# Down projection of a two-layer decoder: ten steps of the second block product moved ahead of the first's last step, other memory for the last sums, final norm of four tiles in halves

## The chip, the cores and the metric

The kernel runs on one core of one Trainium2 chip. The metric is the device time of one execution in microseconds; of several runs the median is taken. The engines are named as in the profile: PE (TensorE matmul), PEld (its weight loads), DVE (VectorE), ACT (ScalarE), POOL (GpSimd) and SP (SyncE, which here only issues DMAs; SPq in the profile's rows).

## The reference

Two decoder layers on a sequence of 1024 rows of width 1024 in float32, each ending in a gated feed-forward block, and a final norm. The attention parts, which the change does not touch, are left out here:

```python
def conv_ffn(h, w_up, conv_w, conv_b, w_down):
    u = h @ w_up                                   # 1024 x 5632
    u = causal_depthwise_conv3(u, conv_w) + conv_b
    a, b = u[..., :D_FF], u[..., D_FF:]            # D_FF = 2816
    return (jax.nn.silu(a) * b) @ w_down           # the down projection
...
for l in range(2):
    ...
    x = x + concat(o_mix, o_mem) @ w_o[l]
    x = x + conv_ffn(rms_norm(x, ffn_norm[l]), w_up[l], conv_w[l], conv_b[l], w_down[l])
return rms_norm(x, final_norm)
```

`rms_norm(x, g)` is x / sqrt(mean(x²) + 1e-6) · g over the 1024 columns of a row.

## The kernel before

**Precision.** A float32 matmul is done as three matmuls on a split of each operand into a high and a low part (`mm3`, lines 157 to 159). The split itself is one ACT instruction (high part, line 81) and one DVE subtraction (low part, line 82). Both operands of the subtraction lie in SBUF.

**The block products.** The down projection is a matrix product in 2x2 blocks done with seven block products instead of eight (the Winograd variant of Strassen's scheme). Class `Down` holds it. Its hidden dimension (2 x 11 tiles of 128) is cut in halves, so each block product has NK = 11 accumulation steps; a step (i, j) is 4 row tiles x 3 matmuls of 128x128x512, 12 matmuls in all. `PRODUCTS` names, for each of the seven products i, the index of its left operand among seven stored factors, its right operand (a tile of `w_down` or a sum of such tiles), whether it adds on into the four running PSUM banks ("chain") or has banks of its own, and which blocks of the output it goes to. Product 0 uses factor 0 and the weights b11; product 1 uses factor 1 and b21. `steps` is the order of all 77 steps: all of product 0, then all of product 1, and so on.

**The left operands.** The gated hidden tiles come out of class `Up` two at a time. `gate` (line 1351, DVE) forms g; `left(k)` (lines 1359 to 1362, POOL) makes for pair k four sums and differences of halves, s1, s2, g12 and s4, into three small tiles (tag `gs`, three buffers) and g itself; `store(k)` (line 1368) writes the seven factors to DRAM with seven DMAs in the order g, h, s2, g12, h12, s1, s4. Factors 0 and 1 are halves of g and h and need no sum. The last pair is k = 10, which step (i, 10) of every product reads.

**Fetch and split.** `fetch` (line 1456) reads the left operands back from DRAM in pairs of steps into a rotating raw buffer (`wr`, three buffers), and stops at a pair whose factors are not stored yet. `prep` splits the operands of a step into four rotating buffers (`wh`, `wl`), three steps ahead of the matmuls. The DMAs of `store`, of `fetch`, of the weights (`claim`, line 1445) and of the rows x (line 1122) are all issued by SP, which works off its queue in order.

**Weight sums.** `sums` makes the sums of weight tiles that later products need, one DVE instruction for each step of products 1 to 4 (lines 1477, 1479, 1481 and the next): `t3 = b22 - b12` belongs to product 1, `b11 = t3 + b11` to product 2, `b12 = b22 - b11` to product 3. Both inputs lie in SBUF.

**The order of instructions.** Inside `Up.run` the order on DVE and ACT is written out by slots; the first seven down steps (slots 160 to 166) and `store(10)` (slot 166) fall in it. Around and after it, a list scheduler fixes each engine's order when the kernel is compiled: it takes the first instruction in program order that its own time model holds to be ready. So a weight sum that is ready can be put in much earlier than the step that it belongs to. On the chip each engine works in that fixed order.

**The end.** `add` (line 1509, DVE) adds the PSUM banks of a finished product to x. Product 6, the last, goes to the left 512 columns of row tiles 4 to 7. `final(t)` is the last norm of row tile t: ACT squares 1024 columns with their sum (line 118), DVE scales the sum (line 119), POOL takes the power -0.5 (line 121), DVE multiplies (line 1094), SP stores 512 KB (line 1095). Its result tile `xn` has three buffers. Tiles 0 to 2 are done during product 5, tiles 3 to 7 after the last step in program order.

Of the kernel before, what the change touches and what calls it, by code (L numbers as in the profile page):

```python
# [8 lines left out]
F32 = mybir.dt.float32  # L9
F32R = mybir.dt.float32r  # L10
BF16 = mybir.dt.bfloat16
AF = mybir.ActivationFunctionType
ALU = mybir.AluOpType
# [4 lines left out]
P = 128  # L18
D = 1024
S = 1024  # L20
NT = S // P
KT = D // P
CH = 512
# [6 lines left out]
NF = DFF // P  # L30
QSC = HD ** -0.5
EPS = 1e-6
# [10 lines left out]
class Trunk:  # L43
    def __init__(self, ctx, tc, a, out):
        self.tc, self.nc, self.a, self.out = tc, tc.nc, a, out
        e = ctx.enter_context
        self.cp = e(tc.tile_pool(name="cp", bufs=1))
        self.wp = e(tc.tile_pool(name="wp", bufs=1))
        self.hp = e(tc.tile_pool(name="hp", bufs=1))
        self.pp = e(tc.tile_pool(name="pp", bufs=1, space=PSUM))  # L50
        self.dp = e(tc.tile_pool(name="dp", bufs=1, space=DRAM))
        self.uid = 0
# [152 lines left out]
    def load_block(self, w, cols, gcol=None, step=2, pool=None):  # L205
        tiles = [self.load_rows(w, k0, min(step, KT - k0), cols, gcol, pool) for k0 in range(0, KT, step)]

        def at(kt, c0, n):
            hi, lo = tiles[kt // step]
            return hi[:, kt % step, c0:c0 + n], lo[:, kt % step, c0:c0 + n]  # L210
        return at
# [230 lines left out]
    def attention(self, ap, l, od, units, work, spare, lead=4, lag=2, lead_work=2):  # L442
# [79 lines left out]
        for k in range(first, len(steps) + lag + 4):  # L522
            st = steps[k] if 0 <= k < len(steps) else None
            run(k, "max")
            if st:
                self.turn_p(ap, st)
            run(k, "exp")
            if st:
                self.lower_p(st)
            run(k, "norm")  # L530
            while items and items[0]["at"] <= k:
                begin(k, items.pop(0))
            if k < 0 and lead_work and items:
                for _ in range(lead_work):
                    if work:
                        advance()
            if st and k < n_fill:
                owed += max(total, 0) / (n_fill - k)
                while owed >= 1 and work:
                    owed -= 1  # L540
                    advance()
            if 0 <= k - lag < len(steps):
                self.value(steps[k - lag])
                if steps[k - lag]["end"]:
                    finish(k, steps[k - lag]["u"])
            if not work and whole and k % 4 == 0:
                operand()
            if k == units[-1]["start"]:
                w_o = self.load_block(self.a["w_o"][l], [(0, CH)])
# [539 lines left out]

    def final(self, pool, gb, t):  # L1090
        nc = self.nc
        xn = self.sb(pool, [P, D], F32, "xn", 3)
        r = self.rstd(pool, self.x[:, t, :], xn)
        nc.vector.scalar_tensor_tensor(xn, self.x[:, t, :], r, gb, ALU.mult, ALU.mult)
        nc.sync.dma_start(self.out[0, t * P:(t + 1) * P, :], xn)

    def residual(self, pool, src):
        self.x = pool.tile([P, NT, D], F32, name=self.nm("x"))
        for t in range(NT):
            self.nc.sync.dma_start(self.x[:, t, :], src[t * P:(t + 1) * P, :])  # L1100
# [11 lines left out]
                up.run(late, down)  # L1112
        return down

    def down_all(self, l, down, pool, each, last):

        self.x = pool.tile([P, NT, D], F32, name=self.nm("x"))
        for n in range(down.at_step, len(down.steps)):
            i, j = down.step()
            if 11 <= n < 27 and n % 2:  # L1120
                t = n // 2 - 5
                self.nc.sync.dma_start(self.x[:, t, :], self.xm[l][t * P:(t + 1) * P, :])
            if i == 5:
                each(j)
            if n == len(down.steps) - 1:
                last()
            if j == down.NK - 1:
                down.add(i)
# [45 lines left out]
    def run(self):  # L1174
        a, tc = self.a, self.tc
        self.constants()
        self.xd = self.dp.tile([S, D], F32, name="xd")
        self.xm = [self.dp.tile([S, D], F32, name=f"xm{l}") for l in range(2)]
        oT = self.layer1_attn(*self.middle(self.layer0()))
        with tc.tile_pool(name="fx1", bufs=1) as fx:  # L1180
            down = self.gated(1, oT, self.xd, fx)
            with tc.tile_pool(name="y1", bufs=1) as yp:
                gb = []

                def each(j):
                    if j == 0:
                        gb.append(self.gain(yp, a["final_norm"].rearrange("(o n) -> o n", o=1)))
                    if j % 3 == 2:
                        self.final(yp, gb[0], j // 3)
                self.down_all(1, down, yp, each, lambda: None)  # L1190
                for t in range(3, NT):
                    self.final(yp, gb[0], t)


class Up:
# [158 lines left out]
    def left(self, k):  # L1354

        g, h = self.hidden[2 * k:2 * k + 2]
        s1, s2, s4 = (self.k.sb(self.late, [P, CH], F32, "gs", 3) for _ in range(3))
        add = self.k.nc.gpsimd.tensor_tensor
        add(s1, g[:, CH:], h[:, CH:], ALU.add)  # L1359
        add(s2, s1, g[:, :CH], ALU.subtract)  # L1360
        add(g[:, CH:], g[:, :CH], g[:, CH:], ALU.subtract)
        add(s4, h[:, :CH], s2, ALU.subtract)
        self.factors = (g[:, :CH], h[:, :CH], s2, g[:, CH:], h[:, CH:], s1, s4)
# [49 lines left out]
class Down:  # L1413

    NK = NF // 2
# [5 lines left out]
    def __init__(self, k, l, gds, fx):  # L1421
        self.k, self.l, self.gds, self.fx = k, l, gds, fx
        self.w = k.a["w_down"][l]
        NK = self.NK
        self.names = {"x": [("b11", i) for i in range(NK)] + [("t3", i) for i in range(NK)] + [("b22", NK - 1)],
                      "h": [("b21", i) for i in range(NK)] + [(n, i) for i in range(NK) for n in ("b12", "b22")][:-1]}
        self.place = {}
        self.steps = [(i, j) for i in range(7) for j in range(NK)]
        self.pairs = [(i, j, min(2, NK - j)) for i in range(7) for j in range(0, NK, 2)]
        self.ready, self.raws, self.at_step = [], [], 0  # L1430

    def claim_x(self):
# [26 lines left out]
    def prep(self, upto):  # L1459

        k = self.k
        while len(self.ready) < min(upto, len(self.steps)):
            i, j = self.steps[len(self.ready)]
            n = self.PRODUCTS[i][1]
            pair = i * (self.NK + 1) // 2 + j // 2
            self.fetch(pair + 1)
            hi, lo = k.whl([P, 2, CH])
            for x, src in enumerate((self.raws[pair][:, j % 2, :], self.place[n, j])):
                k.split(src, hi[:, x, :], lo[:, x, :])
            self.ready.append((hi, lo))  # L1470
            if j % 2 or j == self.NK - 1:
                self.fetch(pair + 4)
# [9 lines left out]
        elif i == 4:  # L1482
            tt(at["b11", j], at["b21", j], at["b11", j], ALU.subtract)

    def step(self):
        k, n = self.k, self.at_step
        i, j = self.steps[n]
        _, _, run, dst = self.PRODUCTS[i]
        self.prep(n + 1 + self.AHEAD)
        if n == 0:  # L1490
            self.chain = [k.psb() for _ in range(4)]
        if j == 0:
            self.banks = self.chain if run else [t[:, x * CH:(x + 1) * CH] for t in (k.psa(), k.psa()) for x in range(2)]
        hi, lo = self.ready[n]
        first = i == 0 or not run
        for p in range(4):
            ps = slice(p * P, (p + 1) * P)
            k.mm3(self.banks[p], (hi[:, 0, ps], lo[:, 0, ps]), (hi[:, 1, :], lo[:, 1, :]), first and j == 0, j == self.NK - 1, not first)
        self.sums(i, j)
        self.at_step += 1  # L1500
        return i, j

    def add(self, i):

        for banks in ((), (self.banks, self.chain))[i] if i < 2 else (self.banks,):
            for p in range(4):
                for rows, col in self.PRODUCTS[i][3]:
                    xs = self.k.x[:, rows * 4 + p, col * CH:(col + 1) * CH]
                    self.k.nc.vector.tensor_tensor(xs, banks[p], xs, ALU.add)
# [57 lines left out]
```

## Time and profile before

| what | value |
|---|---|
| median of 3 runs | 2588.83 us (2588.57 to 2593.57) |
| the profiled execution | 2594.71 us, of which 2592.9 us lie between its first and its last instruction (the span) |
| PE busy | 2467.9 us, 95% of the span |
| DVE, ACT, POOL busy | 1869.4, 1341.3 and 757.6 us |
| granted TensorE clock, mean | 0.986 |

A row of the timeline reads: start in us, busy time in us, engine, line of the kernel, operation, output tile <- input tiles, shapes, how many instructions are merged, and in square brackets how long the engine had been idle before and what ended that. A row of stretches reads: the stretch, its length, the busy time and count of each engine, the granted clock, the share of the DMA engines' time and the rate.

### The profile page before, as it was taken

How to read it: one execution, taken by the hardware profiler on the slowest of the kernel's cores; microseconds unless marked ns; L12 is line 12 of the kernel's file. 1: busy time of each engine (PE TensorE's matmuls, PEld its weight loads, DVE VectorE, ACT ScalarE, POOL GpSimd, SP SyncE). 2: the span in 40 equal slices, each digit the busy share in tenths (PEclk: the TensorE clock that was granted, in tenths of full speed). 3: DMA queues.
4: the chain of work that ended last, by engine and by line, in shares of the span. 5: the costliest groups of instructions: out<-in, count | busy, mean ns of one | idle time of the engine just before them, and what ended most of it. 6: DMA issues, size and time to landing. Idle time of an engine off the chain costs nothing.

```text
span 2592.9 us, 35691 instructions
## 1 busy us (share of the span) xinstructions
PE 2467.9 (95%) x12306; PEld 2058.8 (79%) x12306; DVE 1869.4 (72%) x3172; ACT 1341.3 (52%) x2553; POOL 757.6 (29%) x616
## 2 busy tenths in 40 slices
PE   7899999988999999998999999999999999998998
PEld 7787877777778888886889888887777888886886
DVE  5758888886477878777765468878376777777765
ACT  4437777885254445443454357767144454453443
POOL 0105445453135455433000000000233445544000
PEclk9999999999999999999999999999999999999999
DMA  8473233345323333366235467666522333337433
GB/s 251 141 210 111 66 98 99 110 123 170 108 74 105 96 108 102 98 222 233 90 125 160 147 181 199 190 180 183 195 90 78 102 102 110 106 98 281 165 98 114
DMA packets 302700, 357.68 MB, mean 138 GB/s; under 512 B 37960, under 2 KB 183224, under 8 KB 302520
## 3 DMA queue, kind: packets, MB, share of 16 engines
q1 hardware_dynamic: 302520, 355.41, 43.4%
q8 instruction: 97, 1.59, 0.3%
q14 instruction: 83, 0.68, 0.1%
HBM read 245.55 MB, written 109.78 MB: 137 GB/s over the span
## 4 chain that ended last, share of the span: by engine, by line
PE 74%; DVE 8%; ACT 6%; DMA 5%; POOL 3%; issue 3%; SPq 0%; POOLq 0%; ACTq 0%; DVEq 0%
PE psa L157 12%; PE psa L158 12%; PE psa L159 12%; PE psb L157 9%; PE psb L159 9%; PE psb L158 9%; PE psb L399 4%; PE psb L422 4%; PE psa L300 4%; DVE pt L409 2%; ACT pt L406 1%; POOL gs L1359 1%; DVE wl L82 1%; DMA hT<-in_w_down_dram 1%; DVE ps L330 1%
## 5 line engine op out<-in xcount | busy, mean ns | idle before, releaser
L81 ACT ACTIVATE wh<-wr 128x512 fp32r<-128x512 f32 (+2 forms) x254 | 192.8, 763 | 358.2 <-PE psb L159 146.3
L82 DVE TENSOR_TENSOR wl<-wr,wh 128x512 fp32r<-128x512 f32 (+2 forms) x254 | 242.5, 959 | 166.2 <-ACT wh L81 165.5
L1344 DVE SCALAR_TENSOR_TENSOR v<-u,cw,v 128x1023 f32<-128x1023 f32 (+1 forms) x176 | 275.4, 1565 | 68.8 <-ACT v L1342 67.2
L409 DVE TENSOR_TENSOR pt<-psb,pt 128x512 fp32r<-128x512 f32 (+2 forms) x380 | 247.1, 660 | 66.7 <-ACT pt L406 63.9
L1342 ACT ACTIVATE v<-u,cw 128x1024 f32<-128x1024 f32 x88 | 109.6, 1245 | 310.2 <-DVE u L1331 283.4
L406 ACT ACTIVATE pt<-psb 128x512 fp32r<-128x512 f32 (+2 forms) x380 | 213.4, 572 | 88.0 <-PE psb L399 82.0
L422 PE MATMUL psb<-pt,vv 128*128 128x512 f32 (+2 forms) x864 | 225.9, 356 | 18.2 <-DVE pt L409 12.2
L157 PE MATMUL psa<-hT,wh 128*128 128x512 f32 x560 | 220.3, 394 | 5.3 <-DVE u L1305 5.3
L159 PE MATMUL psa<-hT,wl 128*128 128x512 f32 x560 | 219.5, 392 | 0.8 <-DVE wl L82 0.8
L158 PE MATMUL psa<-hT,wh 128*128 128x512 f32 x560 | 219.7, 392 | 0.0
L300 PE MATMUL psa<-kk,qq 128*128 128x512 f32 (+4 forms) x792 | 185.1, 348 | 13.3 <-DVE stat L330 7.0
L121 POOL TENSOR_TENSOR rs<-ss,consts 128x1 f32<-128x1 f32 x44 | 25.8, 589 | 514.0 <-DVE ss L119 375.0
L422 PEld LDWEIGHTS psb<-pt,vv 128*128 128x128 f32 x864 | 141.2, 191 | 43.5 <-DVE pt L409 21.0
L343 ACT ACTIVATE ps<-ps,stat 128x128 f32<-128x128 f32 (+1 forms) x192 | 147.8, 771 | 46.5 <-DVE stat L330 46.3
L481 POOL TENSOR_TENSOR wr<-wr 128x512 f32<-128x512 f32 x32 | 41.8, 1309 | 430.5 <-DMA kd<-st 246.2
L1246 POOL TENSOR_TENSOR ws<-wr 128x512 f32<-128x512 f32 x44 | 76.5, 1739 | 296.4 <-DMA wr<-in_w_up_dram 256.6
L157 PE MATMUL psb<-wh 128*128 128x512 f32 x352 | 139.5, 396 | 20.8 <-ACT wh L81 20.7
L157 PE MATMUL psb<-hT,wh 128*128 128x512 f32 x384 | 156.6, 408 | 1.5 <-DVE pt L409 1.4
L399 PE MATMUL psb<-consts,ps 128*128 128x128 f32 x928 | 148.4, 277 | 8.1 <-DVE pt L409 3.4
L159 PE MATMUL psb<-hT,wl 128*128 128x512 f32 x384 | 151.1, 393 | 0.0
L158 PE MATMUL psb<-hT,wh 128*128 128x512 f32 x384 | 150.5, 392 | 0.0
L330 DVE CUSTOM_DVE_ANT_0 ps<-psa,caub 128x128 f32<-128x128 f32 (+1 forms) x192 | 139.0, 751 | 14.9 <-PE psa L300 14.7
(286 smaller groups left out, 6799.7 us busy)
## 6 DMA issues: line engine op xcount, KB each, us to landing
wr<-in_w_up_dram SPq DMA_DIRECT2D x88, 512.0 KB
wr<-gd SPq DMA_DIRECT2D x154, 256.0 KB
gd<-v SPq DMA_DIRECT2D x88, 256.0 KB
gd<-gs SPq DMA_DIRECT2D x66, 256.0 KB
o<-ob SPq DMA_DIRECT2D x128, 128.0 KB
wr<-o SPq DMA_DIRECT2D x32, 512.0 KB
hT<-in_w_down_dram SPq DMA_DIRECT2D x64, 256.0 KB
qd<-st SPq DMA_DIRECT2D x56, 256.0 KB
```

Source lines behind the costliest of these rows:

```text
L81: nc.scalar.activation(hi, src, AF.Copy)
L82: nc.vector.tensor_tensor(lo, src, f32(hi), ALU.subtract)
L157: mm(out, lh, rh, start=first, stop=False, skip_group_check=more)
L158: mm(out, lh, rl, start=False, stop=False, skip_group_check=more)
L159: mm(out, ll, rh, start=False, stop=last, skip_group_check=more)
L300: nc.tensor.matmul(out, w, rhs, start=b not in banks[:i], stop=b not in banks[i + 1:])
L330: self.nc.vector.tensor_tensor_reduce(p, s, br["spans"][ii][2], -1.0, 3e38, ALU.add, ALU.min, br["stat"][:, 0, ii:ii + 1])
L399: nc.tensor.transpose(tp[0:kb, x:x + P], br["pt"][ii][:, o:o + kb], self.ident)
L406: nc.scalar.activation(st["hi"], st["src"], AF.Copy)
L409: self.nc.vector.tensor_tensor(st["lo"], st["src"], f32(st["hi"]), ALU.subtract)
L422: self.nc.tensor.matmul(out, v, t, start=st["begin"] and i == 0, stop=st["end"] and i == len(mms) - 1)
L1344: nc.vector.scalar_tensor_tensor(v[:, d:], u[:, :S - d], cw[:, tap, i:i + 1], v[:, d:], ALU.mult, ALU.add)
```

## The change

There are three parts.

1. In `Down`, the steps of products 0 and 1 get a new order: instead of eleven steps of product 0 and then eleven of product 1, there are ten steps of product 0, ten steps of product 1, then (0, 10) and (1, 10). The pairs that `fetch` reads follow the same order (`pairs`, `pair_of`), and the PSUM banks are kept per product. This holds for both layers.
2. In `Up.left`, the last pair's three sums go to two tiles of the tag `ws` instead of three of the tag `gs`. This holds for both layers too.
3. In the last layer only, steps 9 and 10 of product 6 are merged (`joint`): for each row tile the six matmuls of both steps run together. The final norm of tiles 4 to 7 is split: `final_right` squares the right 512 columns and multiplies them by the gain during product 6, and `final_left` does the left 512 columns after the end, scales the finished right half, and stores two halves. `xn` has two buffers instead of three, `final(3)` stands in product 6, and each of tiles 4 to 7 has a buffer of its own.

```diff
     def final(self, pool, gb, t):
-        xn = self.sb(pool, [P, D], F32, "xn", 3)
+        xn = self.sb(pool, [P, D], F32, "xn", 2)
...
+    def final_right(self, pool, gb, t):
+        nc, x = self.nc, self.x[:, t, CH:]
+        xn = self.sb(pool, [P, D], F32, "xr", 4)
+        ss = self.sb(pool, [P, 3], F32, "sr", 4)
+        nc.scalar.activation(xn[:, CH:], x, AF.Square, accum_out=ss[:, 0:1])
+        nc.vector.tensor_scalar(ss[:, 0:1], ss[:, 0:1], 1.0 / D, EPS, ALU.mult, ALU.add)
+        nc.vector.tensor_tensor(xn[:, CH:], x, gb[:, CH:], ALU.mult)
+        return xn, ss
+
+    def final_left(self, pool, gb, t, xn, ss):
+        nc, x = self.nc, self.x[:, t, :CH]
+        nc.scalar.activation(xn[:, :CH], x, AF.Square, accum_out=ss[:, 1:2])
+        nc.vector.scalar_tensor_tensor(ss[:, 2:3], ss[:, 1:2], 1.0 / D, ss[:, 0:1], ALU.mult, ALU.add)
+        r = self.sb(pool, [P, 1], F32, "rs", 4)
+        nc.gpsimd.tensor_tensor(r, ss[:, 2:3], self.nhalf, ALU.pow)
+        nc.scalar.activation(xn[:, CH:], xn[:, CH:], AF.Copy, scale=r)
+        nc.vector.scalar_tensor_tensor(xn[:, :CH], x, r, gb[:, :CH], ALU.mult, ALU.mult)
+        for n in (1, 0):
+            nc.sync.dma_start(self.out[0, t * P:(t + 1) * P, n * CH:(n + 1) * CH], xn[:, n * CH:(n + 1) * CH])
...
-    def down_all(self, l, down, pool, each, last):
+    def down_all(self, l, down, pool, each, last, joint=False, late=None):
...
+        while down.at_step < len(down.steps):
+            n = down.at_step
+            i, j = down.step(joint and n == len(down.steps) - 2)
+            n = down.at_step - 1
...
+            if i == 6 and late:
+                late(j)
...
+                def late(j):
+                    if j == 0:
+                        self.final(yp, gb[0], 3)
+                    if 2 <= j < 6:
+                        halves[j + 2] = self.final_right(yp, gb[0], j + 2)
+                self.down_all(1, down, yp, each, lambda: None, True, late)
+                for t in range(4, NT):
+                    self.final_left(yp, gb[0], t, *halves[t])
...
     def left(self, k):
-        s1, s2, s4 = (self.k.sb(self.late, [P, CH], F32, "gs", 3) for _ in range(3))
+        if k < NF // 2 - 1:
+            s1, s2, s4 = (self.k.sb(self.late, [P, CH], F32, "gs", 3) for _ in range(3))
+        else:
+            two = [self.k.sb(self.pool, [P, 2, CH], F32, "ws", 2) for _ in range(2)]
+            s1, s2, s4 = two[0][:, 0], two[0][:, 1], two[1][:, 0]
...
-        self.steps = [(i, j) for i in range(7) for j in range(NK)]
-        self.pairs = [(i, j, min(2, NK - j)) for i in range(7) for j in range(0, NK, 2)]
+        self.steps = [(i, j) for i in range(2) for j in range(NK - 1)] + [(0, NK - 1), (1, NK - 1)]
+        self.steps += [(i, j) for i in range(2, 7) for j in range(NK)]
+        self.pairs = [(i, j, min(2, NK - j)) for i, j in self.steps if j % 2 == 0]
+        self.pair_of = {(i, j + x): k for k, (i, j, n) in enumerate(self.pairs) for x in range(n)}
...
+        js = (j, j + 1) if joint else (j,)
+        self.prep(n + len(js))
         for p in range(4):
             ps = slice(p * P, (p + 1) * P)
-            k.mm3(self.banks[p], (hi[:, 0, ps], lo[:, 0, ps]), (hi[:, 1, :], lo[:, 1, :]), first and j == 0, j == self.NK - 1, not first)
-        self.sums(i, j)
-        self.at_step += 1
+            for x in js:
+                hi, lo = self.ready[n + x - j]
+                k.mm3(self.banks[i][p], (hi[:, 0, ps], lo[:, 0, ps]), (hi[:, 1, :], lo[:, 1, :]), first and x == 0, x == self.NK - 1, not first)
+        for x in js:
+            self.sums(i, x)
+        self.at_step += len(js)
```

More of the change, by code (lines that the diff above doesn't have):

```diff
@@ L1113, in gated @@
         return down
-    def down_all(self, l, down, pool, each, last):
+    def down_all(self, l, down, pool, each, last, joint=False, late=None):
         self.x = pool.tile([P, NT, D], F32, name=self.nm("x"))
-        for n in range(down.at_step, len(down.steps)):
-            i, j = down.step()
+        while down.at_step < len(down.steps):
+            n = down.at_step
+            i, j = down.step(joint and n == len(down.steps) - 2)
+            n = down.at_step - 1
             if 11 <= n < 27 and n % 2:
@@ L1189, in each @@
                         self.final(yp, gb[0], j // 3)
-                self.down_all(1, down, yp, each, lambda: None)
-                for t in range(3, NT):
-                    self.final(yp, gb[0], t)
+                halves = {}
+                def late(j):
[6 more added lines that the diff above has]
+                    self.final_left(yp, gb[0], t, *halves[t])
 class Up:
@@ L1427, in __init__ @@
         self.place = {}
-        self.steps = [(i, j) for i in range(7) for j in range(NK)]
-        self.pairs = [(i, j, min(2, NK - j)) for i in range(7) for j in range(0, NK, 2)]
+        self.steps = [(i, j) for i in range(2) for j in range(NK - 1)] + [(0, NK - 1), (1, NK - 1)]
+        self.steps += [(i, j) for i in range(2, 7) for j in range(NK)]
+        self.pairs = [(i, j, min(2, NK - j)) for i, j in self.steps if j % 2 == 0]
+        self.pair_of = {(i, j + x): k for k, (i, j, n) in enumerate(self.pairs) for x in range(n)}
+        self.banks = {}
         self.ready, self.raws, self.at_step = [], [], 0
@@ L1464, in prep @@
             n = self.PRODUCTS[i][1]
-            pair = i * (self.NK + 1) // 2 + j // 2
+            pair = self.pair_of[i, j]
             self.fetch(pair + 1)
@@ L1483, in sums, with step @@
             tt(at["b11", j], at["b21", j], at["b11", j], ALU.subtract)
-    def step(self):
+    def step(self, joint=False):
         k, n = self.k, self.at_step
@@ L1492, in step @@
         if j == 0:
-            self.banks = self.chain if run else [t[:, x * CH:(x + 1) * CH] for t in (k.psa(), k.psa()) for x in range(2)]
-        hi, lo = self.ready[n]
+            self.banks[i] = self.chain if run else [t[:, x * CH:(x + 1) * CH] for t in (k.psa(), k.psa()) for x in range(2)]
         first = i == 0 or not run
+        js = (j, j + 1) if joint else (j,)
+        self.prep(n + len(js))
         for p in range(4):
             ps = slice(p * P, (p + 1) * P)
-            k.mm3(self.banks[p], (hi[:, 0, ps], lo[:, 0, ps]), (hi[:, 1, :], lo[:, 1, :]), first and j == 0, j == self.NK - 1, not first)
-        self.sums(i, j)
-        self.at_step += 1
-        return i, j
+            for x in js:
[4 more added lines that the diff above has]
+        self.at_step += len(js)
+        return i, js[-1]
     def add(self, i):
-        for banks in ((), (self.banks, self.chain))[i] if i < 2 else (self.banks,):
+        for banks in ((), (self.banks[1], self.chain))[i] if i < 2 else (self.banks[i],):
             for p in range(4):
```

## The prediction

> **What bounds the kernel now.** I read the page's engine row first, then looked for stretches in which PE does nothing, then asked each engine's timeline what ends them. PE is busy nearly all the time:
>
> ```profile
> PE 2467.9 (95%) x12306; PEld 2058.8 (79%) x12306; DVE 1869.4 (72%) x3172; ACT 1341.3 (52%) x2553; POOL 757.6 (29%) x616
> ```
>
> So only PE's gaps, its half-clock stretches and the end can give anything. The two longest gaps lie in the two down projections, ahead of step (0, 10). The stretches (stretch, length, busy time of the five engines, granted clock, DMA share, GB/s) show each gap, and what follows it:
>
> ```profile
> 1187.40:1197.60 10.20, 0.00 (x0) 0.00 (x0) 0.56 (x1) 0.63 (x2) 5.37 (x4) 0.70 0.57 199
> 1197.65:1201.62 3.97, 3.97 (x9) 3.14 (x10) 3.79 (x7) 3.08 (x6) 0.00 (x0) 0.50 1.04 375
> 2384.05:2394.40 10.35, 0.00 (x0) 0.00 (x0) 0.58 (x2) 0.67 (x2) 5.39 (x4) 0.60 0.56 193
> 2394.40:2399.70 5.30, 5.29 (x12) 4.13 (x13) 4.32 (x7) 3.30 (x6) 0.00 (x0) 0.50 0.93 337
> ...
> 1197.65 0.80 PE L157 MATMUL psb<-wh 128*128 128x512 f32 x1 [10.31 <-ACT wh L81]
> ...
> 2394.41 0.80 PE L157 MATMUL psb<-wh 128*128 128x512 f32 x1 [10.40 <-ACT wh L81]
> ```
>
> PE is empty for 10.31 and 10.40 us and then runs at clock 0.50 for 3.97 and 5.30 us. What ends the gap, in the timelines of POOL, DVE, SP and ACT of the second layer (the first layer's has the same rows 1196.7 us earlier):
>
> ```profile
> 2368.49 17.25 POOL L1359 TENSOR_TENSOR gs<-v,v 128x512 f32<-128x512 f32 x1 [25.22 <-DVE v L1351]
> 2385.82 1.26 POOL L1360 TENSOR_TENSOR gs<-gs,v 128x512 f32<-128x512 f32 x1
> ...
> 1171.83 17.25 POOL L1359 TENSOR_TENSOR gs<-v,v 128x512 f32<-128x512 f32 x1 [25.16 <-DVE v L1351]
> ...
> L1359 POOL TENSOR_TENSOR gs<-v,v x22: 1282/1287/17245, 796.9 to 2368.5; 128x512 f32<-128x512 f32 x22
> ...
> 2374.29 0.69 DVE L82 TENSOR_TENSOR wl<-wr,wh 128x512 fp32r<-128x512 f32 x1
> ...
> 2376.70 0.69 DVE L82 TENSOR_TENSOR wl<-hx,wh 128x512 fp32r<-128x512 f32 x1
> 2377.30 1.90 DVE L1477 TENSOR_TENSOR hx<-hT 128x512 f32<-128x512 f32 x3
> 2379.11 0.69 DVE L1477 TENSOR_TENSOR hx<-hx,hT 128x512 f32<-128x512 f32 x1
> 2379.71 4.91 DVE L1479 TENSOR_TENSOR hx<-hx,hx 128x512 f32<-128x512 f32 x8
> ...
> 2370.38 1.06 SPq L1368 DMA_DIRECT2D gd<-v  x2
> 2387.10 0.32 SPq L1368 DMA_DIRECT2D gd<-gs  x1
> ...
> 2390.46 2.47 SPq L1456 DMA_DIRECT2D wr<-gd  x5
> ...
> 2393.73 0.63 ACT L81 ACTIVATE wh<-wr 128x512 fp32r<-128x512 f32 x1 [17.21 <-DMA wr<-gd]
> ```
>
> The first POOL sum of the last pair, which usually takes 1.29 us, lasts 17.25 us, to 2385.74. DVE's run of weight sums, all with two SBUF inputs and back to back, ends at 2379.71 + 4.91 = 2384.62, which is 1.12 us earlier: POOL gets in only once DVE stops. SP meanwhile stands at the third DMA of the store (2371.44 to 2387.10), and the five fetches behind it, wanted by (0, 10) and by the first steps of product 1, go out at 2390.46. The left operand of (0, 10) itself was stored at 2370.38: PE waits for a queue, not for its data.
>
> **The change part by part.** The sum is against the profiled execution, 2594.71 us (span 2592.9), and is carried to the median, 2588.83; the profiled one lies 5.9 us above it and 1.1 above the slowest run shown. I use its differences only.
>
> *What the gaps cost now.* At full clock a step of 12 matmuls takes 2.72 us:
>
> ```profile
> 2370.45 0.63 ACT L81 ACTIVATE wh<-wr 128x512 fp32r<-128x512 f32 x1 [1.56 <-PE psb L159]
> 2373.17 0.63 ACT L81 ACTIVATE wh<-wr 128x512 fp32r<-128x512 f32 x1 [1.57 <-PE psb L159]
> ```
>
> 2373.17 - 2370.45 = 2.72, 0.227 us a matmul. In the half-clock stretches it is 0.43, so they lose (1 - 0.227/0.43) x 3.97 = 1.87 and x 5.29 = 2.5 us. Lost: 10.31 + 1.87 and 10.40 + 2.5, together 25.1 us.
>
> *The new order.* Before the store, SP now finds the pairs (1, 0) and (1, 2) to fetch, since their factors are long stored; the pair (1, 4) is asked for after step 6, so behind the store. Four DMAs of 256 KB move ahead of it. PE, which ran dry at 2384.01 (2394.41 - 10.40), has four steps more, to 2384.01 + 4 x 2.72 = 2394.9. But POOL is held until DVE stops, and DVE has more to do: the splits of those four steps, and weight sums to fill between them. In the rows above DVE starts one instruction each 0.60 us, so 4.5 in a step's 2.72: two splits and 2.5 sums. The sums left after 2376.70 are four of L1477, ten of L1479 and ten of L1481; ten are needed to fill four steps, so DVE doesn't pause. It first stops where the split of (1, 4) is due and its data isn't there: 18 instructions after 2376.70, 2376.70 + 18 x 0.602 = 2387.5. From DVE's stop to PE's restart it took 2394.41 - 2384.62 = 9.8 us (three more sums on POOL, the stores, the fetch, a split); so PE restarts at 2387.6 + 9.8 = 2397.4. **A gap of 2.5 us stays in each layer** where 10.4 was. It hardly depends on how many pairs are ahead of the store: each moves PE's end and DVE's stop by the same two steps.
>
> *The clock after such a gap* is not in this stretch; the nearest rows are two others:
>
> ```profile
> 693.01 1.26 PE L903 MATMUL psb<-consts,x 128*128 128x128 f32 x8 [1.89 <-DVE x L911]
> 693.05:696.40 3.35, 3.35 (x17) 2.59 (x18) 2.34 (x5) 2.61 (x5) 0.55 (x1) 1.00 0.38 157
> ...
> 1946.36 0.77 PE L157 MATMUL psa<-hT,wh 128*128 128x512 f32 x1 [2.64 <-DVE u L1305]
> 1946.36:1949.70 3.34, 3.34 (x8) 2.67 (x9) 0.45 (x1) 0.00 (x0) 0.00 (x0) 0.50 0.02 5
> ```
>
> After 1.89 us the clock stays at 1.00, after 2.64 us it is 0.50 for at least 3.34 us, worth 3.34 x 0.47 = 1.6. [...]
>
> So each layer's loss becomes 2.5 + 0.8 = 3.3, and the two layers gain 25.1 - 6.6 = **18.5 us**. At the later seams nothing moves: (1, 10) is still followed by (2, 0). The fetch of (0, 10) comes over 10 us after the store.
>
> *The idle tile* gains nothing by itself. POOL's wait ended with `v` of the gate (L1351), and in the last 17 us no store was under way that could hold a `gs` tile; the rate in 40 slices of 1 us from 2370 on:
>
> ```profile
> GB/s 377 389 387 401 219 47 0 0 0 0 0 0 0 0 0 0 0 20 242 315 379 326 326 307 270 344 412 391 309 242 283 51 150 121 219 422 352 266 252 420
> ```
>
> From 2376 to 2387 nothing moves, and POOL's sum ends in the middle of that. Cost bounded by 0 on both sides, as the `ws` tiles are read for the last time at the split of the last up step.
>
> *The end.* The rows from PE's last matmul on:
>
> ```profile
> 2580.22 0.39 PE L159 MATMUL psb<-wh,wl 128*128 128x512 f32 x1
> ...
> 2580.64 0.69 DVE L1509 TENSOR_TENSOR x<-psb,x 128x512 f32<-128x512 f32 x1
> ...
> 2580.36 0.18 ACT L118 ACTIVATION_READ_ACCUMULATOR xn<-x 128x1 f32 x1
> 2580.45 1.04 ACT L118 ACTIVATE xn<-x 128x1024 f32<-128x1024 f32 x1
> ...
> 2585.46 1.06 ACT L118 ACTIVATE xn<-x 128x1024 f32<-128x1024 f32 x1 [2.84 <-DMA out_dram<-xn]
> ...
> 2586.64 0.15 DVE L119 TENSOR_SCALAR ss<-ss 128x1 f32<-128x1 f32 x1 [0.63 <-ACT xn L118]
> 2586.94 0.55 POOL L121 TENSOR_TENSOR rs<-ss,consts 128x1 f32<-128x1 f32 x1 [2.93 <-DVE ss L119]
> 2587.52 1.29 DVE L1094 SCALAR_TENSOR_TENSOR xn<-x,rs,gb 128x1024 f32<-128x1024 f32 x1 [0.73 <-POOL rs L121]
> ```
>
> Tile 7 waits 2.84 us for a buffer that tile 4's store holds, and DVE ends at 2588.81. With a buffer for each tile and half rows, the chain after PE's end (2580.61) is: add 0.69; square of 512 columns, estimated as half of 1.06 plus 0.18 for the sum's read, 0.71; scale 0.15; power 0.55; multiply of 512 columns 0.69, as the add; hand-overs of 0.03 to 0.3 between them, together 0.4. That is 3.2 us, DVE ends at 2583.8, 5.0 earlier. A second DMA ahead of the last costs SP 0.32 (the row of 2387.10), and ACT and DVE may take tile 6's scaling ahead of tile 7's square or sum, 0 to 1.3 (0.62 + 0.69). The halves of the last DMA may give some tenths back. Merging steps 9 and 10 lets the row tiles end six matmuls, 1.36 us, apart instead of 0.68, so that three norms are under way before PE ends; PE's work is the same. I take **4.8**, between 3.5 and 5.3. The right halves (four squares, four multiplies, 0.69 each) lie beside product 6, where a step of 2.72 us has two splits on each of ACT (0.63) and DVE: free. Two `xn` buffers may hold ACT for a store at tiles 2 and 3, covered by the three steps (8.2 us) that it is ahead.
>
> Sum: 18.5 + 4.8 = 23.3; 2594.71 becomes 2571.4, and the median 2588.83 becomes 2565.5, say 2566.
>
> **The rivals.** *A: POOL gets through between DVE's instructions.* [...] In this kernel POOL would then end its four sums near 2376 and SP would never stand long: no gap, 25.1 + 4.8 = 29.9, **2559**. For it: a pause of DVE of some tenths would do, and in the new order ACT's split of (1, 0) may come late. Against: 17.25 us twice, to the hundredth, without getting in, and one pause lets in one of four sums.
>
> *B: the scheduler puts more sums ahead of (1, 4).* If its model has that fetch land late, the 14 remaining sums come first: up to 14 x 0.60 = 8.4 us more, gaps of 2.5 to 10.9 us, with 0.8 to 2.2 for the clock. For it: before, it put 12 sums between 2377.30 and the split of (0, 10). Middle, gaps of 6.7 and 1.6: 25.1 - 16.6 + 4.8 = 13.3, **2575**; the worst gains nothing but 2 to 5 at the end, 2585.
>
> *C: the order does nothing.* If SP has the pairs of product 1 behind the store, PE runs dry where it did: only the end gains, **2584**.
>
> *D: slower, by the two `xn` buffers.* ACT is in order, and a square that waits for a store holds the splits behind it. Before, with three buffers, this was
>
> ```profile
> 2533.09 1.06 ACT L118 ACTIVATE xn<-x 128x1024 f32<-128x1024 f32 x1 [0.56 <-DMA out_dram<-xn]
> ...
> 2582.76 2.61 DMA out_dram<-xn
> ```
>
> If each of tiles 0 to 3 waited for a fetch's turn on SP (two steps, 5.44) and a store (2.61, the second row, from the chain), 32 us less the cover of 8.2 and a cold window 1.6 more: 25.6 against 23.3, **2591**. It decides from 31.5 us of waiting on; the trace shows 0.56.
>
> **How the numbers follow.** Forecast 0.59 (gaps of 2 to 4 us, its own range 2562 to 2571), A 0.14, B 0.18, C 0.06, D 0.03. The three runs before differ by 0.2% at most; 0.2% (5.2 us) is about what can be told from no change. Faster by more: the forecast, A and nearly all of B, 0.90; within: C and B's end, 0.07; slower 0.03. The range runs from below A, 2557, to past B's middle, 2577, and leaves out some 0.17.
>
> **What would show it.** Right: L1359 of the last pair still over 17 us long and ending 1.1 us after a DVE run of L82, L1477 and L1479; PE's gap of 2 to 4 us moved to after step (1, 3); no wait ahead of (0, 10); fetches between the weights' DMAs and `gd<-v` on SP; from PE's last matmul to the span's end 7.5 us instead of 12.3. Wrong: L1359 of 1.3 us (A), a gap of 6 us or more behind a row of L1481 (B), a gap ahead of (1, 0) instead of (1, 4) (C), or ACT idle behind `out_dram<-xn` with PE waiting (D).

## The result, and the profile after

The changed kernel takes 2576.01 us (median of 4 runs, 2570.72 to 2579.85) beside 2590.49 for the kernel before in the same comparison (2588.57 to 2593.57): ratio 0.9933, 95% interval 0.9916 to 0.995, 14.5 us less. The forecast was 2566, 23.3 less: right in sign and inside the wide range (2557 to 2577), but only by 1 us, and outside the forecast's own 2562 to 2571. The gain is 9 us smaller than forecast. The wide range reached that far up for the sake of rival B, which the rows below do not show; that the time still fell inside it is partly luck. The profiled execution took 2576.98 us, its span is 2574.9.

POOL's timeline of the changed kernel around the last pair's sums, first layer and then second:

```profile
1182.38 20.27 POOL L1396 TENSOR_TENSOR ws<-v,v 128x512 f32<-128x512 f32 x1 [25.18 <-DVE v L1384]
...
2366.92 4.02 POOL L1396 TENSOR_TENSOR ws<-v,v 128x512 f32<-128x512 f32 x1 [25.18 <-DVE v L1384]
2371.01 1.63 POOL L1397 TENSOR_TENSOR ws<-ws,v 128x512 f32<-128x512 f32 x1
...
2374.30 1.74 POOL L1399 TENSOR_TENSOR ws<-v,ws 128x512 f32<-128x512 f32 x1
```

The two layers, which run the same instructions, went differently. In the first, POOL's first sum is shut out and lasts 20.27 us, as forecast; in the second it takes 4.02. The first layer on DVE, SP, ACT and PE:

```profile
1200.21 1.30 DVE L1519 TENSOR_TENSOR hx<-hx,hx 128x512 f32<-128x512 f32 x2
1211.28 0.69 DVE L82 TENSOR_TENSOR wl<-wr,wh 128x512 fp32r<-128x512 f32 x1 [9.78 <-ACT wh L81]
...
1184.02 2.31 SPq L1496 DMA_DIRECT2D wr<-gd  x4
1186.68 0.99 SPq L1405 DMA_DIRECT2D gd<-v  x2
1204.05 0.32 SPq L1405 DMA_DIRECT2D gd<-ws  x1
...
1207.17 3.17 SPq L1496 DMA_DIRECT2D wr<-gd  x6
...
1210.62 0.63 ACT L81 ACTIVATE wh<-wr 128x512 fp32r<-128x512 f32 x1 [11.54 <-DMA wr<-gd]
1211.16 0.62 ACT L81 ACTIVATE wh<-hT 128x512 fp32r<-128x512 f32 x1
...
1211.82 0.67 PE L157 MATMUL psa<-wh 128*128 128x512 f32 x1 [3.06 <-ACT wh L81]
```

The stretches of PE's gap and of what follows it:

```profile
1208.77:1211.82 3.05, 0.00 (x0) 0.00 (x0) 0.54 (x1) 1.20 (x3) 0.00 (x0) 1.00 0.92 289
1211.99:1215.41 3.42, 3.28 (x8) 2.22 (x9) 3.42 (x6) 3.02 (x6) 0.00 (x0) 0.50 1.02 395
```

From 1182.76 on DVE runs through (1201.51 - 1182.76)/0.60 = 31 two-input instructions without a pause and stops at 1201.51; POOL's sum ends 1.14 us later. SP now has four fetches ahead of the store, stands in the store until 1204.05, and fetches on at 1207.17. PE's gap is 3.06 us where it was 10.31, and the clock is 0.50 for 3.42 us behind it. The second layer has no gap at all; DVE's timeline shows what let POOL in:

```profile
2369.09 0.69 DVE L1517 TENSOR_TENSOR hx<-hT 128x512 f32<-128x512 f32 x1
2369.86 1.62 DVE L82 TENSOR_TENSOR wl<-wr,wh 128x512 fp32r<-128x512 f32 x1
2371.41 1.78 DVE L82 TENSOR_TENSOR wl<-hx,wh 128x512 fp32r<-128x512 f32 x1
```

DVE starts one instruction each 0.60 us; the split at 2369.86 comes 0.77 after its predecessor, 0.17 late. It starts when ACT's high part of the same operand ends, at 2369.84; in the first layer the high part of the same split is done at 1184.97 and DVE comes to it at 1185.16. POOL is in from then on, the two take turns (1.6 to 1.8 us for an instruction of either), and all four sums are done at 2376.04.

The first matmul behind the next seam, before and after, gives the gain of each layer, measured from the start of POOL's first sum:

```profile
1233.08 0.47 PE L157 MATMUL psa<-wh 128*128 128x512 f32 x1 [0.62 <-DVE x L1509]
2430.45 0.47 PE L157 MATMUL psa<-wh 128*128 128x512 f32 x1 [0.62 <-DVE x L1509]
```

```profile
1236.39 0.47 PE L157 MATMUL psa<-wh 128*128 128x512 f32 x1 [0.63 <-DVE x L1553]
2415.78 0.47 PE L157 MATMUL psa<-wh 128*128 128x512 f32 x1 [0.63 <-DVE x L1553]
```

First layer: 1233.08 - 1171.83 = 61.25 before, 1236.39 - 1182.38 = 54.01 after, 7.2 gained. Second: 2430.45 - 2368.49 = 61.96 and 2415.78 - 2366.92 = 48.86, 13.1 gained. The end, PE's last matmul first, then DVE:

```profile
2565.59 0.39 PE L159 MATMUL psb<-wh,wl 128*128 128x512 f32 x1
...
2566.93 0.75 DVE L1115 SCALAR_TENSOR_TENSOR xr<-x,rs,gb 128x512 f32<-128x512 f32 x1 [0.73 <-POOL rs L1113]
2567.60 0.69 DVE L1553 TENSOR_TENSOR x<-psb,x 128x512 f32<-128x512 f32 x1
...
2569.08 0.75 DVE L1115 SCALAR_TENSOR_TENSOR xr<-x,rs,gb 128x512 f32<-128x512 f32 x1 [0.73 <-POOL rs L1113]
2569.75 0.15 DVE L1111 SCALAR_TENSOR_TENSOR sr<-sr 128x1 f32<-128x1 f32 x1
2570.63 0.75 DVE L1115 SCALAR_TENSOR_TENSOR xr<-x,rs,gb 128x512 f32<-128x512 f32 x1 [0.73 <-POOL rs L1113]
```

From PE's end (2565.98) to the span's end (2574.93) it is 8.95 us; before, 2592.88 - 2580.61 = 12.28. That is 3.3 gained. The three add up to 23.6, very near the forecast of 23.3, and yet the median gained only 14.5. Two things stand between. First, this one execution was lucky in one layer. Second, it reached the last pair of the first layer 10.55 us later than the profile of before (1182.38 against 1171.83), although every engine has the same instructions in the same order up to there. Some 5 us of that came back in the second layer's attention: its first sum starts 1.57 us earlier than before, where 10.55 - 7.2 = 3.3 later was to be expected. The profiles of the experiments with the same order up to there start the first layer's sum anywhere between 1171.83 and 1182.38.

Much of that difference is the clock. Between 560 and 770 us, in the first layer's attention, the stretches of the kernel before and of the changed kernel are

```profile
560.00:770.00 210.00, 194.11 (x1006) 157.35 (x1004) 133.30 (x241) 100.31 (x205) 72.34 (x71) 0.99 0.36 121
560.00:770.00 210.00, 191.64 (x977) 156.60 (x976) 134.79 (x242) 99.92 (x208) 69.37 (x69) 0.96 0.37 121
```

The mean clock of 0.99 over these 210 us is one stretch of 3.41 us at half clock (751.1 to 754.5), that of 0.96 is three of 3.41 (from 570.3, 703.4 and 761.4) and one of 6.82 (from 628.3). From the start to the last pair of the first layer PE works for 13.6 us at half clock before and for 28.2 in the changed kernel, and it is idle for 68.2 and 72.2 us. By the prediction's 0.47 the clock makes 6.9 us of difference and the idle time 4.0, together 10.9 where 10.55 was measured. It isn't shown to be the change's doing: in the twelve profiles PE works between 9.9 and 31.9 us at half clock up to there, and the kernel with all three parts and the sums on DVE has the least. So single profiles can't be subtracted as a whole here; stages can.

### The profile page after: what moved, and what is told of

It reads as the page before. It is cut to its first block, busy times and chain, and to the rows that moved or that the text cites. A ratio compares the mean times of both kernels' runs of the same rounds, so it can differ in the third digit from the quotient of the medians.

```text
span 2574.9 us, 35712 instructions
## 1 busy us (share of the span) xinstructions
PE 2467.4 (96%) x12306; PEld 2059.2 (80%) x12306; DVE 1880.5 (73%) x3180; ACT 1347.7 (52%) x2565; POOL 745.7 (29%) x616
## 4 chain that ended last, share of the span: by engine, by line
PE 74%; DVE 8%; ACT 6%; DMA 5%; issue 3%; POOL 3%; SPq 1%; POOLq 0%; ACTq 0%; DVEq 0%
PE psa L157 12%; PE psa L158 12%; PE psa L159 12%; PE psb L157 9%; PE psb L159 9%; PE psb L158 9%; PE psa L300 4%; PE psb L399 4%; PE psb L422 4%; ACT pt L406 2%; DVE pt L409 2%; ACT ps L343 1%; DVE wl L82 1%; DVE ps L330 1%; POOL ws L1396 1%
## 5 line engine op out<-in xcount | busy, mean ns | idle before, releaser
L1279 POOL TENSOR_TENSOR ws<-wr 128x512 f32<-128x512 f32 x44 | 72.2, 1640 | 295.6 <-DMA wr<-in_w_up_dram 243.3
L300 PEld LDWEIGHTS psa<-kk,qq 128*128 128x128 f32 x792 | 123.0, 195 | 31.2 <-DVE stat L330 10.0
```

The lines of the kernel that those rows point to most:

```text
L300: nc.tensor.matmul(out, w, rhs, start=b not in banks[:i], stop=b not in banks[i + 1:])
```

## The experiments

My theory: POOL is shut out by DVE's unbroken run of instructions with two SBUF inputs; the new order doesn't shorten that, it only gives PE four more steps to live on. Each edit is against the kernel before unless it says otherwise.

**The three parts, one at a time.** *Part 1 alone*, the order of steps:

```diff
-        self.steps = [(i, j) for i in range(7) for j in range(NK)]
+        self.steps = [(i, j) for i in range(2) for j in range(NK - 1)] + [(0, NK - 1), (1, NK - 1)]
+        self.steps += [(i, j) for i in range(2, 7) for j in range(NK)]
```

> Part 1 alone: the new order of steps, with the old buffers for the last sums and the old final norm. Theory (POOL's first sum of the last pair is shut out while DVE runs two-SBUF-input instructions back to back, and the new order only gives PE four steps of cover): in each layer PE's gap is either about 2.5 to 3 us (POOL's sum some 20 us long) or none (a pause of DVE lets POOL in, sum of some 4 us), as in the two layers of the changed kernel's profile; 17 to 25 us faster than before. Rival 1 (it was the idle tile that let POOL in, in the second layer): the sum is over 17 us long in both layers again, gaps of 2.5 to 3 us in both, about 16 to 18 us faster. Rival 2 (the order doesn't matter, the end does): no change beyond 2 us.

2582.58 us beside 2595.07 (ratio 0.995, 0.9931 to 0.9969): 12.5 us, less than the 17 to 25 that I expected. Both layers are shut out, as rival 1 has it, which leaves that rival open here; part 2 alone and the second profile of the whole change, both below, speak against it. The gap stands behind step (1, 3) with 3.22 and 3.40 us. POOL's first sum over the whole kernel (the list by tile: ns, least, median and greatest), and the second layer's restart in PE's timeline:

```profile
L1392 POOL TENSOR_TENSOR gs<-v,v x22: 1289/1290/20285, 803.1 to 2362.4; 128x512 f32<-128x512 f32 x22
```

```profile
2392.22 0.79 PE L157 MATMUL psa<-wh 128*128 128x512 f32 x1 [3.40 <-ACT wh L81]
```

*Part 3 alone*, the end in halves (joined steps, `final_right`, `final_left`):

> Part 3 alone: steps 9 and 10 of the last product merged and the final norm of tiles 4 to 7 in halves, with the old order and the old buffers. From the changed kernel's profile: from PE's last matmul to the end of the span 8.9 us instead of 12.3, 3.4 us faster. By the prediction's term: 7.5 us, 4.8 us faster. The gaps of 10.3 and 10.4 us ahead of step (0, 10) stay, with POOL's sum at 17.25 us.

2590.01 us beside the same 2595.07 (ratio 0.9984, 0.9972 to 0.9995), 8.94 us from PE's last matmul to the end, gaps of 10.27 and 10.41 as before. *Part 2 alone*, the last pair's sums in `ws` tiles:

> Part 2 alone (the last pair's sums go to the idle ws tiles), with the old order. My theory: nothing holds a gs tile in that stretch, so POOL waits as long as before, its first sum takes 17 us in both layers, both gaps stay at 10 us: ratio 1.000 within 0.0015. Rival: another tile gets POOL in sooner, as seen once with the whole change, where layer 1's sum took 4.02 us; then at least one layer loses its gap and this kernel is 10 us or more faster, ratio 0.996 or less.

2593.57 beside 2594.94 (ratio 0.9999, 0.9987 to 1.0011). POOL's first sum takes 17.23 us in both layers; the second layer's row is

```profile
2364.95 17.23 POOL L1363 TENSOR_TENSOR ws<-v,v 128x512 f32<-128x512 f32 x1 [25.18 <-ACT wh L81]
```

The idle tile does nothing. The product of the three ratios, 0.995 x 0.9984 x 0.9999 = 0.9933, is that of the whole change, though the intervals are too wide to make much of the agreement.

**Was the 4.02 us of the second layer the change's doing?** The changed kernel again, unedited:

> The changed kernel once more, beside the others on one chip. Its program is fixed, so POOL's first sum of the last pair can differ from run to run only by the small time differences of the engines. In the first profile it was 20.27 us long in the first layer and 4.02 us in the second; in the kernel with the new order alone both layers had a gap of over 3 us, and its runs fell in two groups, near 2574 and near 2583. Theory (POOL gets in by luck, at a pause of some tenths): runs spread over 8 us or more, and another profile may show another pair of outcomes; the mean gain is 14 to 22 us. Rival (the idle tile is what lets POOL in, in the second layer): the second layer's sum is near 4 us again.

2576.44 us beside 2593.01 (ratio 0.9935, 0.992 to 0.995). This time POOL is shut out in both layers (POOL and PE):

```profile
1182.38 20.28 POOL L1396 TENSOR_TENSOR ws<-v,v 128x512 f32<-128x512 f32 x1 [25.20 <-DVE v L1384]
...
2366.47 20.28 POOL L1396 TENSOR_TENSOR ws<-v,v 128x512 f32<-128x512 f32 x1 [25.18 <-DVE v L1384]
...
1212.18 0.79 PE L157 MATMUL psa<-wh 128*128 128x512 f32 x1 [3.42 <-ACT wh L81]
2396.13 0.74 PE L157 MATMUL psa<-wh 128*128 128x512 f32 x1 [3.28 <-ACT wh L81]
```

The stretches behind both gaps:

```profile
1212.20:1215.60 3.40, 3.39 (x7) 2.40 (x8) 3.40 (x7) 3.04 (x6) 0.00 (x0) 0.50 1.04 387
1215.60:1219.00 3.40, 3.40 (x10) 2.60 (x10) 3.40 (x7) 0.92 (x2) 0.00 (x0) 0.56 0.89 343
...
2396.20:2399.60 3.40, 3.33 (x7) 2.31 (x8) 3.40 (x7) 3.00 (x6) 0.00 (x0) 0.50 1.02 387
2399.60:2403.00 3.40, 3.40 (x16) 2.79 (x15) 3.40 (x7) 1.15 (x2) 0.00 (x0) 1.00 0.94 334
```

The same program gives 4.02 or 20.28 us in the same place: whether a pause of 0.17 us falls into DVE's run differs from execution to execution. It may be why the runs of part 1 alone lie in two groups (2573.71 and 2574.66; four from 2582.49 to 2584.97), as a layer that gets through is worth some 6 us more than one that doesn't; only the profiled runs show the layers, so this isn't shown. The clock is a rival: the two short runs had mean clocks of 0.990 and 0.993, the four long ones 0.986 to 0.990, and the 17 runs of the kernel before beside them go from 2587.87 us at 0.988 to 2601.24 at 0.984 with no change of program at all.

**Take the cause away.** Old order, but the last pair's four sums on DVE, so POOL has nothing to wait for:

```diff
-        add = self.k.nc.gpsimd.tensor_tensor
+        add = (self.k.nc.gpsimd if k < NF // 2 - 1 else self.k.nc.vector).tensor_tensor
```

> The kernel before, with the four sums of the last pair on DVE instead of POOL, all else as it was. Theory: nothing shuts them out, four DVE instructions of 0.60 us end by about 2372, SP goes on, the gap ahead of (0, 10) is gone: 25 us faster, without any new order. Rival (the sums wait for a buffer or for a store): the wait moves to DVE with them, and the gap stays: no change or slower.

2568.92 us (ratio 0.9907, 0.989 to 0.9924), no gap in either layer. One line gains 26 us, more than the whole change. Now the other way round: sums left on POOL and DVE held to program order in products 0 to 4, so that no weight sum stands early between the splits:

```diff
-            i, j = down.step()
+            if n < 55:
+                with self.tc.manual_schedule(engines={mybir.EngineType.DVE}):
+                    i, j = down.step()
+            else:
+                i, j = down.step()
```

> The kernel before, with DVE's order in products 0 to 4 held to program order: the weight sums are done with their own steps instead of ahead of them, so DVE pauses in each step of product 0 after its two splits. The same work on every engine, POOL's sums still on POOL, old order of steps. Theory: POOL gets in at the first pause, its four sums take 1.3 to 3 us each, the gap is gone or under 2 us: 22 to 25 us faster. Rival (POOL's 17 us are a wait for a buffer or store, or a slow POOL): they stay, no change. Second rival (the early sums were needed early): gaps appear in products 1 to 3, slower.

2567.53 us (ratio 0.9905, 0.9888 to 0.9922), no gap, and on POOL and DVE of the second layer

```profile
2353.45 3.43 POOL L1363 TENSOR_TENSOR gs<-v,v 128x512 f32<-128x512 f32 x1 [24.74 <-DVE v L1355]
...
2356.54 0.88 DVE L82 TENSOR_TENSOR wl<-wr,wh 128x512 fp32r<-128x512 f32 x1 [0.82 <-ACT wh L81]
```

The gain is 27.5 us. The sum on POOL ends at 2356.88, which is 1.16 us after DVE's run before the pause had ended (2355.72); in the shut-out layers it was 1.12 and 1.14 us. Both sides of the pair are shown: without POOL's sum or without DVE's run the loss is gone, in the old order of steps.

**Is it the pause, or the kind of instruction?** The rival to "POOL needs an idle DVE" is "POOL needs one DVE instruction that doesn't read two SBUF tiles". So old order, DVE as busy as before or busier, and a small reduction with one input after each split of steps 6 to 10:

```diff
                 k.split(src, hi[:, x, :], lo[:, x, :])
+                if 6 <= len(self.ready) <= 10:
+                    k.nc.vector.reduce_sum(k.sb(k.cp, [P, 1], F32, "door", 2), f32(lo[:, x, 0:2]), axis=AX.X)
```

> The kernel before, with one short DVE instruction with a single SBUF input (a sum of two columns into one, some 0.1 us) added after each split of steps 6 to 10 of each down projection; its result is used by nothing. DVE has more work, no pause, and the sums stay on POOL and in the old order. Theory, narrow form (POOL is shut out by a run of two-SBUF-input instructions, and any other instruction between two of them lets it in): POOL's four sums end by about 2377, the gap of 10 us is gone or under 2 us, 22 to 25 us faster. Rival (POOL needs DVE to be idle for some tenths): POOL's first sum stays at 17 us or more, no change.

2576.71 us beside 2593.01 (ratio 0.9938, 0.9925 to 0.9952). POOL, DVE and PE of the second layer, and the stretch behind PE's gap:

```profile
2360.95 2.22 POOL L1359 TENSOR_TENSOR gs<-v,v 128x512 f32<-128x512 f32 x1 [25.19 <-DVE v L1351]
...
2361.93 0.15 DVE L1471 TENSOR_REDUCE door<-wl 128x1 f32<-128x2 f32 x1
2362.00 1.72 DVE L82 TENSOR_TENSOR wl<-hx,wh 128x512 fp32r<-128x512 f32 x1
...
2376.93 4.29 DVE L1481 TENSOR_TENSOR hx<-hx,hx 128x512 f32<-128x512 f32 x7
2381.15 0.68 DVE L82 TENSOR_TENSOR wl<-wr,wh 128x512 fp32r<-128x512 f32 x1
...
2381.88 0.73 PE L159 MATMUL psb<-wh,wl 128*128 128x512 f32 x2 [2.98 <-DVE wl L82]
...
2381.88:2385.28 3.40, 3.40 (x15) 2.80 (x16) 3.40 (x8) 1.15 (x2) 0.00 (x0) 1.00 0.68 169
```

DVE doesn't pause, and one reduction of 0.15 us lets POOL in: its first sum takes 2.22 us where it was 17.25, in both layers. So POOL didn't need an idle DVE here; one instruction of another kind between two of the run was enough (whether a long one would do as well wasn't tried). The gain is 16.3 us, not the 22 to 25 that I expected: of the gap 2.98 us stays in each layer, now for another reason, as the split of (0, 10) stands behind seven weight sums that the scheduler put ahead of it. A gap of 1.01 us, some 12 us earlier, is new. Sums ahead of the split are what rival B described, here in the old order; they weren't seen in the new one.

**What is the new order worth once nothing is shut out?** The changed kernel with the last pair's sums on DVE, and the old order with the sums on DVE and part 3:

> The changed kernel with the four sums of the last pair on DVE instead of POOL. Theory: no gap in either layer whatever the luck, so the two projections gain the full 25 us and the end its 3.4: 28 us faster than before, 4 to 9 us faster than the changed kernel, with a smaller spread. If the new order has a use of its own beside POOL's shut-out, it is faster than the kernel before with the sums on DVE (which gained 25) by more than the 3.4 us of the end; if not, by just that.

> The kernel before with part 3 (the end in halves) and with the last pair's four sums on DVE; the order of the steps is the old one. If the new order only covers the time in which POOL is shut out, it has nothing to cover once POOL makes no sums: this kernel then equals the one with all three parts and the sums on DVE, about 26 to 29 us under the kernel before, ratio 0.9890 to 0.9905, with no gap at either seam. Rival: the new order is worth something by itself (its three steps' lead saves fetches or cold windows elsewhere); then this one lies 3 us or more above the kernel with all three parts and the sums on DVE, ratio 0.991 or more.

2564.09 beside 2593.01 (ratio 0.9895, 0.9879 to 0.991) with the new order, 2566.44 beside 2594.94 (ratio 0.9892, 0.9872 to 0.9911) with the old one; neither has a gap there. The new order is worth nothing that can be measured by itself: it only paid for part of the wait. The first of the two is 12 us faster than the changed kernel on the same chip, more than the 4 to 9 that I expected, and its spread is hardly smaller (8.2 us against 9.2).

**The end.** The same kernel as the first of these two, and at the end DVE's and ACT's order written out: the add of tile t, then the sum for t - 1, then the multiply of t - 2.

```diff
-                for t in range(4, NT):
-                    self.final_left(yp, gb[0], t, *halves[t])
+                with self.tc.manual_schedule(engines={mybir.EngineType.DVE, mybir.EngineType.Activation}):
+                    for t in range(4, NT + 2):
+                        if t < NT:
+                            down.add_tile(t - 4)
+                        if 5 <= t < NT + 1:
+                            rs[t - 1] = self.final_sum(yp, t - 1, *halves[t - 1])
+                        if t >= 6:
+                            self.final_left(yp, gb[0], t - 2, halves[t - 2][0], rs[t - 2])
```

> As the one before (last pair's sums on DVE), and with the order of DVE and ACT after the last matmul written out: the add of the next row tile stands ahead of the multiply of the one before it, and the sum of the last tile ahead of the multiply of the one before. In the changed kernel DVE waited 0.73 us for POOL ahead of each multiply, with the next add behind it, and the last add began 1.6 us after its matmuls had ended. Theory (the end is bound by this order): from PE's last matmul to the end of the span 6.6 us instead of 8.9, about 30.5 us faster than before. Rival (the end is bound by the eight stores): 8.5 us or more, no gain from the order.

2563.79 us (ratio 0.9893, 0.9877 to 0.9909), the lowest median here, though not measurably ahead of the one without this edit (2564.09). The last rows of PE, DVE and SP:

```profile
2560.62 0.39 PE L159 MATMUL psb<-wh,wl 128*128 128x512 f32 x1
...
2561.05 0.69 DVE L1562 TENSOR_TENSOR x<-psb,x 128x512 f32<-128x512 f32 x1
...
2564.18 0.75 DVE L1120 SCALAR_TENSOR_TENSOR xr<-x,rs,gb 128x512 f32<-128x512 f32 x1 [0.44 <-POOL rs L1113]
...
2560.56 5.44 SPq L1122 DMA_DIRECT2D out_dram<-xr  x8
```

The last add now starts 0.04 us after PE's end and DVE ends 3.92 after it (5.40 in the changed kernel), but the span ends 8.26 after it (8.95; 9.51 in the kernel without this edit). So of 1.5 us saved on DVE 0.7 to 1.3 arrive; the rest goes to what follows DVE's last end, which is the last stores (4.33 us from there to the span's end where it was 3.55 and 4.11). My 6.6 us was a miss: I had counted the chain of arithmetic, not the stores behind it. The rival, which put the end at 8.5 us or more, came nearer.

## Why the prediction was right, and where it was off

**Right, by its steps.** Counted from the start of POOL's first sum, the prediction had DVE stop at 2387.5 - 2368.49 = 19.0 us and PE run dry at 2394.9 - 2368.49 = 26.4. Measured in the first layer: 1201.51 - 1182.38 = 19.1 and 1208.77 - 1182.38 = 26.4. The gap is behind step (1, 3); nothing waits ahead of (0, 10); SP's four fetches stand between the weights' DMA and the store; the idle tile is worth 0; the order alone leaves two gaps and the end alone leaves both old ones. The two `xn` buffers (D) cost nothing visible: part 3 alone came out faster.

**The term "9.8 us from DVE's stop to PE's restart" was too short.** It was 1211.82 - 1201.51 = 10.3 us. POOL, store and fetch took what they did before (the fetch goes out 5.66 us after DVE's stop, 5.84 before). But before, (0, 10) lacked only its left operand, and PE started when one split was done; here ACT, held in its order by the missing factor, had the split of the weights of (1, 4) (`wh<-hT` at 1211.16) behind it, 0.54 us more. The gaps are 3.06 to 3.42 instead of 2.5.

**The clock was the larger miss.** I took 0.8 a gap, an estimate of mine between the 0 and the 1.6 of the prediction's two rows (2.5 by the long gaps). No run shows that 0.8: behind the gaps of 2.98 to 3.42 us there was no half clock, one stretch of it (1.6) or two (3.0). The five gaps of 3.06 to 3.42 us in the two profiles of the changed kernel and the one of part 1 alone were all followed by half clock: three of them by one stretch of about 3.4 us, worth 3.42 x 0.47 = 1.6, and the two longest, 3.40 and 3.42, by two in a row. In the rows of the second profile the clock behind the gap of 3.42 us is 0.50 and then 0.56, which makes half clock from PE's restart at 1212.18 to about 1218.6, worth 6.4 x 0.47 = 3.0 and beyond that 1.6. So 0.8 was too small for gaps of this length, and it was short by more the longer the gap came out. That isn't a rule for every gap near 3 us: both gaps of 2.98 us in the run with the reduction were followed by clock 1.00, and so was, in the profile of part 2 alone, the gap of 2.64 us at the place of the program that the prediction quotes at 0.50 (1.00 from 1945.75 to 1949.10). The length of a gap alone doesn't settle it: ahead of the same matmul a gap of 2.89 us was followed by clock 0.50 for 3.40 us in the kernel before (at 116.20) and by 1.00 in the changed kernel (at 117.80). What else settles it isn't shown.

By layer, both terms together: shut-out layers gained 7.2 (first profile), 5.6 and 7.8 (second profile: 1238.07 and 2420.62 at the seam, rows below), instead of 9.25. With the gaps and the clock just priced, and what the gaps cost before (12.2 and 12.9 us), the gains would be 12.2 - 3.1 - 1.6 = 7.5 in the first profile, and 12.2 - 3.4 - 3.0 = 5.8 and 12.9 - 3.3 - 1.6 = 8.0 in the second: these two terms leave no more than 0.3 us of a layer open.

```profile
1238.07 0.47 PE L157 MATMUL psa<-wh 128*128 128x512 f32 x1 [0.62 <-DVE x L1553]
2420.62 0.47 PE L157 MATMUL psa<-wh 128*128 128x512 f32 x1 [0.62 <-DVE x L1553]
```

Their mean, 6.9, twice, and 3.3 for the end are 17.0 us; the medians say 14.5 and 16.6 (intervals 13 to 22 and 13 to 21). So some 5 us of the forecast's excess are gap and clock, 1.5 the end, and the rest lies within the runs' scatter. The layer that escaped would raise the sum: with it the four layers gain 8.4 on average, and 20.2 us in all, more than either median shows. What takes the difference isn't shown; half clock elsewhere in the kernel is of that size.

**The end: 4.8 forecast, 3.3 measured.** I had DVE end 3.2 us after PE; it was 5.40. The scheduler put tile 5's multiply, which waits 0.73 us for POOL's power, ahead of the last add, which so started 1.6 us after PE's end (2567.60 against 2565.98), and tile 6's multiply ahead of tile 7's sum, another 0.7. I had bounded that mix-up at 1.3. The written order shows the cause for DVE's end, 3.92 with it gone; at the span's end only a part of that arrived.

**Rivals.** A came true in one layer of one profile, though the first sum took 4.02 us there and not the 1.3 that A names. In that profile's first layer POOL was kept out by 31 DVE instructions running, which stood back to back for 18.75 us (1182.76 to 1201.51); in the run with the reduction one DVE instruction of 0.15 us between two of them let it in. How the one engine keeps the other out isn't shown. The argument against A, that one pause lets in one of four sums, was wrong: after the pause of 0.17 us all four got through by taking turns with DVE. The longer gaps of B and the gap ahead of (1, 0) of C came in neither profile of the changed kernel.

## What to carry to other kernels

When one POOL instruction lasts ten times its usual time, look at DVE for the same stretch: here an unbroken run of instructions with two SBUF inputs shut POOL out for 17.23 to 20.28 us where the sum usually takes 1.29, and the cheap cures (move the sums, keep the list scheduler from filling the run, put in one short one-input instruction) gained 26, 27.5 and 16 us, where making room for the wait by the new order gained 12.5. A gap that is shortened and not closed can still pay for the clock (1.6 or 3.0 us behind the gaps of 3.06 to 3.42 us here), so price what remains both without and with one or two stretches at half clock. And where two layers run the same code and one is much better, run it again before calling it an effect.

## What the hardware showed that I had not expected

A small DVE instruction was long beside POOL's, too. One on 128x4 elements in the first layer's attention of the changed kernel, with POOL's rows of the same time, and then the same DVE instruction in the kernel before:

```profile
566.91 3.48 DVE L354 TENSOR_SCALAR stat<-stat 128x4 f32<-128x4 f32 x1
567.32 0.61 POOL L362 TENSOR_TENSOR pc<-pc,stat 128x256 f32<-128x256 f32 x1
567.89 2.48 POOL L481 TENSOR_TENSOR wr<-wr 128x512 f32<-128x512 f32 x2
```

```profile
564.07 0.45 DVE L354 TENSOR_SCALAR stat<-stat 128x4 f32<-128x4 f32 x1
```

It took 3.48 us, until POOL's three instructions were through, against 0.45. The second profile of the changed kernel (3.48) and that of part 3 alone (3.49) show the long form, that of part 2 alone (0.46) the short one, and up to there all of them have the same instructions in the same order. That POOL's instructions are the cause was not tested. At this place it makes up 3 of the 10.55 us; the larger part of them is half clock, as said above.
